# Gates and branch projections of a mixer: from features on the partitions to tokens on the partitions

## The chip, the cores and the metric

One core of a Trainium2 chip runs the whole program. The metric is the device time of one execution in microseconds; the time of a kernel is the median of its runs.

## The reference

The model has three blocks on 256 tokens of width 1024, all in float32. The change lies in the third, whose mixer adds up four branches, each projected and gated:

```python
h = _rms_norm(x, norm_mix_pre[l])
(a_q, a_k, a_v, f_q, f_k, f_v, f_g, c_u, s_x, s_b, s_c) = jnp.split(h @ w_in[l], cuts, axis=-1)
...
ya = (_rms_norm(ya, diff_norm[l]) * (1.0 - lambda_init)).reshape(B, S, BR_W)
...
c_a, c_g = jnp.split(c_u + b_glu[l], 2, axis=-1)
yc = _dwconv_causal(c_a * jax.nn.sigmoid(c_g), conv_dw[l]) + conv_dw_b[l]
yc = jax.nn.silu(_layer_norm(yc, conv_ln_g[l], conv_ln_b[l]))

ys = s_b * _dwconv_causal(s_c * s_x, sc_w[l])

br = jnp.stack([ya, yf, yc, ys], axis=2)
proj = jnp.einsum('bsnc,ncd->bsnd', br, w_branch[l])
gates = jax.nn.sigmoid(h @ w_gate[l] + b_gate[l]).reshape(B, S, N_BRANCH, D)
mixed = jnp.sum(gates * proj, axis=2) @ w_out[l]
x = x + _rms_norm(mixed, norm_mix_post[l])
```

Lines of three dots stand for what is left out: the two attentions that give `ya` and `yf`. Each branch is 512 wide (BR_W), D is 1024; `w_gate` is 1024x4096, split into four gates of 1024, and `w_branch` is 4x512x1024. The branches are counted n = 0 to 3 in the order of the stack, so the convolution is n = 2.

## The kernel before, in words

All weights come from one array in the order in which they are used (`weight_order`). A chunk is 1 MB in two pieces of 128x1024; `feed` loads pieces on SP's queue some pieces ahead. Products are exact to float32: `prepare` rounds each piece to a high half on ScalarE (`whi`, line 156), the rest to a low half on VectorE (`wlo`, line 162), and `mm3` (lines 235 to 237) multiplies high by high, low by high and high by low. How far ahead pieces are prepared is limited by `nprep` (11 in this stage) past twice the chunks that `done()` has counted.

Nothing is scheduled by the compiler: the order of the instructions on each engine is the order in which the program writes them. A step of work on TensorE ends with a `tick`, which writes, in this order, the `whi` of the next piece, one step of each generator in `lanes` and `light`, the `wlo` of that piece, and some steps of `slow`. With lanes alive or fewer than three pieces waiting one piece is prepared in a tick, otherwise two; `slow` advances by three steps, by one if lanes are alive or two pieces were prepared, and by one after a branch.

There are two ways to multiply. `ws` keeps the weights as the stationary operand, 128 output features, and streams the 256 tokens: the result has features on the partitions. `as_` keeps 128 tokens as the stationary operand and streams 512 features of weights: the result has tokens on the partitions. `as_pair` runs a pair of chunks through `as_`, first for the one half of the tokens and then for the other, and calls `evac` for each half; it ticks four times, and counts its chunks as done in the second half.

The stage in question runs over MIX_STEPS. `gates(j)` computes two gate tiles of 128 features by `ws_chunk` (48 matmuls of 256 columns); ScalarE takes them out of PSUM with Sigmoid, the bias being a value of each partition (line 1183). `branches(j0)` projects four tiles of 128 features with one chunk; for each two of them VectorE multiplies the result in PSUM with the gates (lines 1205 and 1207) and adds it up in `part` (line 1208). With the last branch, n = 2, the sum is split into high and low half for the product with `w_out_2`, whose stationary operand has features on the partitions. PSUM results live in a pool of four banks (`bank`), the weights and most activations in a pool of 43 buffers of 4 KB (`b4`).

Beside it, VectorE works through the convolution: `conv_taps` in `slow`, 31 taps on each of four tiles, two tiles at a time (line 860). After the fifth branch chunk `conv_lane` is started, which waits for the taps to run out, transposes the result on TensorE, normalizes it on VectorE, transposes it back, applies Silu on ScalarE and splits it: that is branch n = 2. After the sixth, `mem_norm` loads the memory on POOL's queue (`mem_load`), normalizes it and transposes it, for a later stage.

Of the kernel before, what the change touches and what calls it, by code (L numbers as in the profile page):

```python
# [37 lines left out]
PP = {}  # L38
_o = 0
for _n, _w in (("b_glu", 8), ("conv_dw", 4 * 31), ("conv_dw_b", 4), ("ln_g", 4), ("ln_b", 4),  # L40
               ("sc_w", 12), ("b_gate", 32), ("ffn_dw", 3 * 44), ("ffn_dw_b", 44)):
    PP[_n] = _o
    _o += _w
NPP = _o
# [55 lines left out]
def tile_model(ctx: ExitStack, tc: tile.TileContext, order, wall, x, mem, gains, pparam, rparam, w_fg,  # L100
# [721 lines left out]
    def ppc(name, i, n=1):  # L822
        return pp[:, PP[name] + i:PP[name] + i + n]
# [317 lines left out]


    sbt = None
    for i in range(4):
        if i % 2 == 0:
            sbt = t2("sb")
            ws_chunk(("colsat", "w_in_2", S_B + i * 128), lambda ps: nc.scalar.activation(sbt, ps, AF.Copy))

        def shortconv(ps, i, sbt):
            sx = t1("sx")  # L1150
            nc.scalar.activation(sx, ps[:, 0:256], AF.Copy)
            nc.vector.tensor_tensor(sx, ps[:, 256:512], sx, op=ALU.mult)
            y = t1("sy")
            k0 = PP["sc_w"] + i * 3
            nc.vector.tensor_scalar(y, sx, pp[:, k0 + 2:k0 + 3], None, op0=ALU.mult)
            for s in (1, 2):
                nc.vector.scalar_tensor_tensor(y[:, s:256], sx[:, 0:256 - s], pp[:, k0 + 2 - s:k0 + 3 - s], y[:, s:256],
                                               op0=ALU.mult, op1=ALU.add)
            yield
            if i == 0:  # L1160
                br(3)
            nc.vector.tensor_tensor(y, y, sbt[:, (i % 2) * 256:(i % 2) * 256 + 256], op=ALU.mult)
            split(brh[3][:, i, :], brl[3][:, i, :], y)

        def evac(ps):
            lane(shortconv(ps, i, sbt))

        ws_chunk(("list256", "w_in_2", S_X + i * 128, S_C + i * 128), evac)


    gbuf, part, mx = {}, [], {}
    state["branch"] = 0

    def gates(j):

        if j // 2 % 2 == 0:
            gbuf["tile", j // 4] = b4([128, 4, 256], "gates")
        tile = gbuf["tile", j // 4]

        def evac(ps):  # L1180
            for f in range(2):
                n, ft = GATE_ORDER[j + f]
                nc.scalar.activation(tile[:, (j + f) % 4, :], ps[:, f * 256:f * 256 + 256], AF.Sigmoid, bias=ppc("b_gate", n * 8 + ft))
        ws_chunk(("gates", j), evac)

    def branches(j0, count=4):

        if j0 % 4 == 0:
            gbuf["w"] = weights(("branch", j0))
        w = gbuf["w"]  # L1190
        for j in range(j0, j0 + count):
            n, ft = GATE_ORDER[j]
            if j % 2 == 0:
                gbuf["ps"] = bank("ps_br")
            ps = gbuf["ps"][:, (j % 2) * 256:(j % 2) * 256 + 256]
            ws(ps, w, (j % 4) * 128, lambda k: brh[n][:, k, :], lambda k: brl[n][:, k, :], width=512)
            if j % 4 == 3:
                done()
            if j % 2 == 0:
                continue  # L1200
            g = gbuf["tile", j // 4].rearrange("p a b -> p (a b)")[:, (j % 4 - 1) * 256:(j % 4 + 1) * 256]
            ft -= 1
            m = part[ft // 4].rearrange("p a b -> p (a b)")[:, ft % 4 * 256:ft % 4 * 256 + 512]
            if n == 0:
                nc.vector.tensor_tensor(m, gbuf["ps"], g, op=ALU.mult)
            else:
                nc.vector.tensor_tensor(g, gbuf["ps"], g, op=ALU.mult)
                nc.vector.tensor_tensor(m, m, g, op=ALU.add)
            if n == 2:
                a = mx[ft // 2] = act_pair()  # L1210
                split(a[0], a[1], tiles(m, 256))
            tick(taps=1)


    mth, mtl, memn = {}, {}, []
# [28 lines left out]

    for kind, j in MIX_STEPS:
        if kind == "gate":
            gates(j)
            if j == 6:
                drain(*lanes, *light)
                part.extend(b4([128, 4, 256], f"part{i}") for i in range(2))  # L1250
            if j == 30:
                drain(cl)
        else:
            branches(j)
            if j == 16:
                cl = lane(conv_lane())
            if j == 20:
                ml = lane(mem_norm(mem_load()))
    drain(ml)
    acc = [pair("mix0"), pair("mix1")]  # L1260
    items = [(weights(("rows2", "w_out_2", c)), *mx.pop(c)) for c in range(4)]


    xk = {}
# [156 lines left out]

GATE_ORDER = [(n, ft + f) for ft in range(0, 8, 2) for n in (0, 1, 3) for f in range(2)] + [(2, ft) for ft in range(8)]
MIX_STEPS = [("gate", 0), ("gate", 2), ("gate", 4), ("gate", 6)]
for _c in range(6):
    MIX_STEPS += [("branch", 4 * _c)] + [("gate", 4 * _c + 8 + _i) for _i in (0, 2) if 4 * _c + 8 + _i < 24]
MIX_STEPS += [("gate", _j) for _j in (24, 26, 28, 30)] + [("branch", 24), ("branch", 28)]


def weight_order():
# [37 lines left out]

    for kind, j in MIX_STEPS:  # L1470
        if kind == "gate":
            o.append(("gates", j))
        else:
            o.append(("branch", j))
    o.extend(("rows2", "w_out_2", c) for c in range(4))
# [18 lines left out]
def _chunk(inp, key):  # L1494
# [24 lines left out]
    if kind == "ffn512":  # L1519
# [1 line left out]
        w = inp["w_up_2"][c * 512:c * 512 + 512]  # L1521
        w = np.concatenate([w[:, n * 256:n * 256 + 256], w[:, D_FF2 + n * 256:D_FF2 + n * 256 + 256]], axis=1)
        return w.reshape(4, 128, 512).transpose(1, 0, 2)
    if kind == "gates":
        w = np.concatenate([inp["w_gate_2"][:, n * 1024 + ft * 128:n * 1024 + ft * 128 + 128]
                            for n, ft in GATE_ORDER[key[1]:key[1] + 2]], axis=1)
        return w.reshape(8, 128, 256).transpose(1, 0, 2)
    if kind == "branch":
        w = np.concatenate([inp["w_branch_2"][n, :, ft * 128:ft * 128 + 128]
                            for n, ft in GATE_ORDER[key[1]:key[1] + 4]], axis=1)  # L1530
        return w.reshape(4, 128, 512).transpose(1, 0, 2)
    raise KeyError(key)


def _layout(inp):

    def per(v):
        return v.reshape(-1, 128).T

    def taps(w):  # L1540
        k, c = w.shape
        return w.reshape(k, c // 128, 128).transpose(2, 1, 0).reshape(128, -1)

    pparam = np.concatenate([per(inp["b_glu_2"]), taps(inp["conv_dw_2"]), per(inp["conv_dw_b_2"]),
                             per(inp["conv_ln_g_2"]), per(inp["conv_ln_b_2"]), taps(inp["sc_w_2"]),
                             per(inp["b_gate_2"]), taps(inp["ffn_dw_2"]), per(inp["ffn_dw_b_2"])], axis=1)
    rparam = np.concatenate([inp[n] for n in ("b_fgt_2", "diff_norm_2", "lam_q1_2", "lam_q2_2", "lam_k1_2",
                                              "lam_k2_2")])[None, :]
    gains = np.stack([inp[n] for n in GAINS])
    return gains, pparam, rparam, inp["w_in_2"][:, F_G:F_G + 8]  # L1550


# [36 lines left out]
```

## Time and profile before

| | us |
|---|---|
| three runs: median (lowest to highest) | 1264.73 (1264.48 to 1264.80) |
| the profiled execution, its own time | 1264.71 |
| its span, first to last instruction | 1263.0 |
| TensorE busy | 1237.4 (98%) |
| VectorE busy | 877.7 (69%) |
| ScalarE busy | 678.4 (54%) |
| GpSimd busy | 9.3 (1%) |
| TensorE's granted clock, mean | 0.999 |

The busy times come from one profiled execution. Matmuls overlap in the pipeline: a matmul of 256 columns is shown with 283 ns although the next one starts 120 ns after it, so the pace is read from the starts. A wait is given in brackets at the end of a line of the timeline, with the engine and the tile that ended it.

### The profile page before, as it was taken

How to read it: one execution, taken by the hardware profiler on the slowest of the kernel's cores; microseconds unless marked ns; L12 is line 12 of the kernel's file. 1: busy time of each engine (PE TensorE's matmuls, PEld its weight loads, DVE VectorE, ACT ScalarE, POOL GpSimd, SP SyncE). 2: the span in 40 equal slices, each digit the busy share in tenths (PEclk: the TensorE clock that was granted, in tenths of full speed). 3: DMA queues.
4: the chain of work that ended last, by engine and by line, in shares of the span. 5: the costliest groups of instructions: out<-in, count | busy, mean ns of one | idle time of the engine just before them, and what ended most of it. 6: DMA issues, size and time to landing. Idle time of an engine off the chain costs nothing. (4 is left out here: it accounts for less than half of the span.)

```text
span 1263.0 us, 20014 instructions
## 1 busy us (share of the span) xinstructions
PE 1237.4 (98%) x7870; PEld 1115.1 (88%) x7870; DVE 877.7 (69%) x1537; ACT 678.4 (54%) x1103; POOL 9.3 (1%) x22
## 2 busy tenths in 40 slices
PE   6999999999999999999999999999999999999997
PEld 4888888899988888899998999899999897899996
DVE  6774768755566766765557578688877877588773
ACT  5553445644444765654444545754446575666552
POOL 0000000000000000000000000000000000000000
PEclk9999999999999999999999999999999999999999
DMA  9765564665664535566565644255665564455530
GB/s 342 279 186 156 159 218 166 213 196 178 198 217 134 183 120 180 187 214 190 179 211 181 208 144 141 71 174 170 188 203 197 182 207 163 159 191 185 183 117 34
DMA packets 64206, 227.43 MB, mean 180 GB/s; under 512 B 8048, under 2 KB 8304, under 8 KB 64112
## 3 DMA queue, kind: packets, MB, share of 16 engines
q1 hardware_dynamic: 61808, 217.76, 52.8%
q0 software_dynamic: 2304, 8.39, 2.0%
q8 instruction: 62, 1.02, 0.3%
q14 instruction: 32, 0.26, 0.1%
HBM read 225.08 MB, written 1.05 MB: 179 GB/s over the span
## 5 line engine op out<-in xcount | busy, mean ns | idle before, releaser
L162 DVE TENSOR_TENSOR wlo<-raw,whi 128x1024 fp32r<-128x1024 f32 x406 | 480.1, 1220 | 79.9 <-ACT whi L156 78.8
L156 ACT ACTIVATE whi<-raw 128x1024 fp32r<-128x1024 f32 x406 | 406.8, 1049 | 52.8 <-PE ps_ws L237 14.8
L235 PE MATMUL ps_ws<-xhi,whi 128*128 128x256 f32 x1376 | 391.3, 284 | 1.2 <-ACT fpT L1126 0.9
L236 PE MATMUL ps_ws<-xlo,whi 128*128 128x256 f32 x1376 | 389.3, 283 | 0.0
L237 PE MATMUL ps_ws<-xhi,wlo 128*128 128x256 f32 x1376 | 389.3, 283 | 0.0
L235 PEld LDWEIGHTS ps_ws<-xhi,whi 128*128 128x128 f32 x1376 | 263.8, 192 | 5.9 <-issue 2.5
L236 PEld LDWEIGHTS ps_ws<-xlo,whi 128*128 128x128 f32 x1376 | 263.9, 192 | 1.5
L237 PEld LDWEIGHTS ps_ws<-xhi,wlo 128*128 128x128 f32 x1376 | 263.9, 192 | 0.0
L235 PE MATMUL ps_as<-whi,xhi 128*128 128x512 f32 x352 | 142.2, 404 | 0.3 <-ACT xhi L231 0.3
L236 PE MATMUL ps_as<-wlo,xhi 128*128 128x512 f32 x352 | 137.7, 391 | 0.5 <-DVE wlo L162 0.5
L237 PE MATMUL ps_as<-whi,xlo 128*128 128x512 f32 x352 | 138.1, 392 | 0.0
L268 PE MATMUL mlp<-wlo,act 128*128 128x512 f32 x240 | 93.7, 390 | 0.0
L267 PE MATMUL mlp<-whi,act 128*128 128x512 f32 x240 | 93.5, 390 | 0.0
L237 PEld LDWEIGHTS ps_as<-whi,xlo 128*128 128x128 f32 x352 | 66.2, 188 | 15.3 <-DVE xlo L232 1.1
L236 PEld LDWEIGHTS ps_as<-wlo,xhi 128*128 128x128 f32 x352 | 66.5, 189 | 14.2 <-DVE wlo L162 1.3
L235 PEld LDWEIGHTS ps_as<-whi,xhi 128*128 128x128 f32 x352 | 66.4, 189 | 13.6 <-ACT xhi L231 0.9
L662 DVE SCALAR_TENSOR_TENSOR relu<-ps_ws,relu 128x512 f32<-128x512 f32 x24 | 16.6, 691 | 87.1 <-ACT relu L661 87.1
L661 ACT ACTIVATE relu<-ps_ws 128x512 f32<-128x512 f32 x24 | 14.4, 598 | 113.8 <-PE ps_ws L237 113.8
L271 PE MATMUL mlp<-whi,act 128*128 128x512 f32 x240 | 73.9, 389 | 0.0
L271 PEld LDWEIGHTS mlp<-whi,act 128*128 128x128 f32 x240 | 45.1, 188 | 9.5
L267 PEld LDWEIGHTS mlp<-whi,act 128*128 128x128 f32 x240 | 45.2, 188 | 8.6
L268 PEld LDWEIGHTS mlp<-wlo,act 128*128 128x128 f32 x240 | 45.2, 188 | 8.6
(427 smaller groups left out, 1613.8 us busy)
## 6 DMA issues: line engine op xcount, KB each, us to landing
raw<-in_wall_dram SPq DMA_DIRECT2D x406, 512.0 KB, 4.2
h<-in_x_dram SPq DMA_DIRECT2D x4, 256.0 KB, 5.7
gainln_mix_post<-in_gains_dram POOLq DMA_DIRECT2D x2, 512.0 KB, 5.6
gainln_mlp_pre<-in_gains_dram POOLq DMA_DIRECT2D x2, 512.0 KB, 6.7
gainln_mlp_post<-in_gains_dram POOLq DMA_DIRECT2D x2, 512.0 KB, 7.6
mem<-in_mem_dram POOLq DMA_DIRECT2D x2, 512.0 KB, 5.8
out_dram<-h SPq DMA_DIRECT2D x4, 256.0 KB, 2.9
dec<-in_t_dec_dram SPq DMA_DIRECT2D x2, 384.0 KB, 8.9
```

The lines of the kernel that those rows point to most:

```text
L156: nc.scalar.activation(hi, raw, AF.Copy)
L162: nc.vector.tensor_tensor(lo, raw, hi.bitcast(F32), op=ALU.subtract)
L235: nc.tensor.matmul(o, ah, bh, start=start, stop=False)
L236: nc.tensor.matmul(o, ah, bl, start=False, stop=False)
L237: nc.tensor.matmul(o, al, bh, start=False, stop=stop)
L267: nc.tensor.matmul(acc[t][n], ah[:, k, ts], wh[k][:, ns], start=st, stop=False)
L268: nc.tensor.matmul(acc[t][n], ah[:, k, ts], wl[k][:, ns], start=False, stop=False)
L271: nc.tensor.matmul(acc[t][n], al[:, k, ts], wh[k][:, ns], start=False, stop=False)
L661: nc.scalar.activation(r, ps, AF.Relu)
L662: nc.vector.scalar_tensor_tensor(r, ps, 0.0, r, op0=ALU.max, op1=ALU.mult)
```

## The change

The gates and the branch projections change from `ws` to `as_`. A gate group is now 512 features of one branch for 256 tokens, from two chunks, by `as_pair`; a branch group is 512 features of one branch from one chunk. The number of chunks is the same, 16 and 8, and so is the order of gates and branches; `GATE_ORDER` now names halves of 512 features instead of tiles of 128.

With the features in the free dimension, the gate's bias is no longer one value for each partition. It comes as a row, broadcast to 128 partitions by a DMA on POOL's queue (`gate_bias`, two groups for each DMA; the rows stand behind the gains in `gains`), VectorE adds it while it takes the result out of PSUM, and ScalarE applies Sigmoid in SBUF. VectorE multiplies the projection with the gate as before, now for one half of the tokens at a time; the additions into `part` go to GpSimd. For the product with `w_out_2` the sum has to have features on the partitions: `mixed` transposes it on TensorE, four tiles of 128x128 for each half of the tokens and of the features, and splits it out of PSUM. It is put into `light` and runs one tick later.

```diff
@@ -1141,7 +1141,17 @@
 
 
     sbt = None
+    gbias = {}
+
+    def gate_bias(j):
+
+        b = gbias[j // 2] = b4([128, 2, 512], "gate_bias")
+        r = len(GAINS) + j // 2
+        nc.gpsimd.dma_start(b, gains[r:r + 1, :].rearrange("a (n c) -> a n c", n=2).broadcast_to([128, 2, 512]))
+
     for i in range(4):
+        if i == 2:
+            gate_bias(0)
         if i % 2 == 0:
             sbt = t2("sb")
             ws_chunk(("colsat", "w_in_2", S_B + i * 128), lambda ps: nc.scalar.activation(sbt, ps, AF.Copy))
@@ -1168,48 +1178,50 @@
         ws_chunk(("list256", "w_in_2", S_X + i * 128, S_C + i * 128), evac)
 
 
-    gbuf, part, mx = {}, [], {}
-    state["branch"] = 0
-
-    def gates(j):
-
-        if j // 2 % 2 == 0:
-            gbuf["tile", j // 4] = b4([128, 4, 256], "gates")
-        tile = gbuf["tile", j // 4]
-
-        def evac(ps):
-            for f in range(2):
-                n, ft = GATE_ORDER[j + f]
-                nc.scalar.activation(tile[:, (j + f) % 4, :], ps[:, f * 256:f * 256 + 256], AF.Sigmoid, bias=ppc("b_gate", n * 8 + ft))
-        ws_chunk(("gates", j), evac)
-
-    def branches(j0, count=4):
-
-        if j0 % 4 == 0:
-            gbuf["w"] = weights(("branch", j0))
-        w = gbuf["w"]
-        for j in range(j0, j0 + count):
-            n, ft = GATE_ORDER[j]
-            if j % 2 == 0:
-                gbuf["ps"] = bank("ps_br")
-            ps = gbuf["ps"][:, (j % 2) * 256:(j % 2) * 256 + 256]
-            ws(ps, w, (j % 4) * 128, lambda k: brh[n][:, k, :], lambda k: brl[n][:, k, :], width=512)
-            if j % 4 == 3:
+    gbuf, part, mx = {}, {}, {}
+
+    def gate_group(j):
+
+        if j % 2 == 0 and j < 6:
+            gate_bias(j + 2)
+        tile = gbuf[j] = b4([128, 2, 512], "gates")
+
+        def evac(t, ps):
+            nc.vector.tensor_tensor(tile[:, t, :], ps, gbias[j // 2][:, j % 2, :], op=ALU.add)
+            nc.scalar.activation(tile[:, t, :], tile[:, t, :], AF.Sigmoid)
+
+        as_pair([("cols512", "w_gate_2", 2 * GATE_ORDER[j][1] + GATE_ORDER[j][0], c) for c in range(2)], evac)
+
+    def branch_group(j):
+
+        f, n = GATE_ORDER[j]
+        w = weights(("branch", j))
+        g = gbuf.pop(j)
+        if n == 0:
+            part[f] = b4([128, 2, 512], "part")
+        m = part[f]
+        for t in range(2):
+            ps = bank("ps_br")
+            as_(ps, w, brh[n], brl[n], t, True, True)
+            if n == 0:
+                nc.vector.tensor_tensor(m[:, t, :], ps, g[:, t, :], op=ALU.mult)
+            else:
+                nc.vector.tensor_tensor(g[:, t, :], ps, g[:, t, :], op=ALU.mult)
+                nc.gpsimd.tensor_tensor(m[:, t, :], m[:, t, :], g[:, t, :], op=ALU.add)
+            if t == 1:
                 done()
-            if j % 2 == 0:
-                continue
-            g = gbuf["tile", j // 4].rearrange("p a b -> p (a b)")[:, (j % 4 - 1) * 256:(j % 4 + 1) * 256]
-            ft -= 1
-            m = part[ft // 4].rearrange("p a b -> p (a b)")[:, ft % 4 * 256:ft % 4 * 256 + 512]
-            if n == 0:
-                nc.vector.tensor_tensor(m, gbuf["ps"], g, op=ALU.mult)
-            else:
-                nc.vector.tensor_tensor(g, gbuf["ps"], g, op=ALU.mult)
-                nc.vector.tensor_tensor(m, m, g, op=ALU.add)
             if n == 2:
-                a = mx[ft // 2] = act_pair()
-                split(a[0], a[1], tiles(m, 256))
+                if t == 0:
+                    mx[2 * f], mx[2 * f + 1] = act_pair(), act_pair()
+                later(lambda t=t: mixed(f, t))
             tick(taps=1)
+
+    def mixed(f, t):
+        pt = bank("ps_mx")
+        transposes(pt, part[f][:, t, :])
+        for c in range(2):
+            a = mx[2 * f + c]
+            split(a[0][:, :, tok(t)], a[1][:, :, tok(t)], tiles(pt[:, c * 256:c * 256 + 256]))
 
 
     mth, mtl, memn = {}, {}, []
@@ -1244,21 +1256,20 @@
 
     for kind, j in MIX_STEPS:
         if kind == "gate":
-            gates(j)
-            if j == 6:
+            gate_group(j)
+            if j == 1:
                 drain(*lanes, *light)
-                part.extend(b4([128, 4, 256], f"part{i}") for i in range(2))
-            if j == 30:
+            if j == 7:
                 drain(cl)
         else:
-            branches(j)
-            if j == 16:
+            branch_group(j)
+            if j == 4:
                 cl = lane(conv_lane())
-            if j == 20:
+            if j == 5:
                 ml = lane(mem_norm(mem_load()))
     drain(ml)
     acc = [pair("mix0"), pair("mix1")]
-    items = [(weights(("rows2", "w_out_2", c)), *mx.pop(c)) for c in range(4)]
+    items = [(weights(("rows2", "w_out_2", c)), *mx[c]) for c in range(4)]
 
 
     xk = {}
@@ -1421,11 +1432,11 @@
 
 
 
-GATE_ORDER = [(n, ft + f) for ft in range(0, 8, 2) for n in (0, 1, 3) for f in range(2)] + [(2, ft) for ft in range(8)]
-MIX_STEPS = [("gate", 0), ("gate", 2), ("gate", 4), ("gate", 6)]
-for _c in range(6):
-    MIX_STEPS += [("branch", 4 * _c)] + [("gate", 4 * _c + 8 + _i) for _i in (0, 2) if 4 * _c + 8 + _i < 24]
-MIX_STEPS += [("gate", _j) for _j in (24, 26, 28, 30)] + [("branch", 24), ("branch", 28)]
+GATE_ORDER = [(f, n) for f in range(2) for n in (0, 1, 3)] + [(f, 2) for f in range(2)]
+MIX_STEPS = [("gate", 0), ("gate", 1)]
+for _j in range(6):
+    MIX_STEPS += [("branch", _j)] + ([("gate", _j + 2)] if _j < 4 else [])
+MIX_STEPS += [("gate", 6), ("gate", 7), ("branch", 6), ("branch", 7)]
 
 
 def weight_order():
```

## Rows read from the trace of the kernel before

**Rows 1.** The page's first part: busy time, share of the span, instructions by engine.
```profile
PE 1237.4 (98%) x7870; PEld 1115.1 (88%) x7870; DVE 877.7 (69%) x1537; ACT 678.4 (54%) x1103; POOL 9.3 (1%) x22
```

**Rows 2.** Busy times by stretch, gates to `w_out_2`: length, engines, clock, DMA.
```profile
843.40:866.40 23.00, 23.00 (x194) 23.00 (x193) 20.37 (x37) 11.29 (x17) 0.00 (x0) 1.00 0.58 178
866.40:929.60 63.20, 63.20 (x529) 63.20 (x528) 53.47 (x87) 27.18 (x36) 0.00 (x0) 1.00 0.60 179
929.60:986.40 56.80, 56.26 (x468) 55.61 (x468) 40.90 (x69) 33.77 (x55) 2.09 (x4) 1.00 0.59 200
```

**Rows 3.** Timeline, TensorE, in a gate chunk: start, length, engine, line, what.
```profile
950.09 0.28 PE L237 MATMUL ps_ws<-xhi,wlo 128*128 128x256 f32 x1
950.21 0.28 PE L235 MATMUL ps_ws<-xhi,whi 128*128 128x256 f32 x1
```

**Rows 4.** Timeline, TensorE, retention stage: twelve 512-column matmuls, then four transposes between such.
```profile
60.00 0.39 PE L235 MATMUL ps_as<-whi,xhi 128*128 128x512 f32 x1
...
62.72 0.39 PE L235 MATMUL ps_o<-vh,ph 128*128 128x512 f32 x1
...
66.81 0.60 PE L294 MATMUL ps_ot<-ident,og 128*128 128x128 f32 x4
67.16 0.48 PE L235 MATMUL ps_as<-whi,xhi 128*128 128x512 f32 x1
67.48 0.40 PE L236 MATMUL ps_as<-wlo,xhi 128*128 128x512 f32 x1
```

**Rows 5.** Instructions on tile `part`: count, min/median/max ns, first and last start.
```profile
L1205 DVE TENSOR_TENSOR part<-ps_br,gates x4: 684/684/693, 870.9 to 941.6; 128x512 f32<-128x512 f32 x4
L231 ACT ACTIVATE act<-part x4: 632/632/634, 980.0 to 992.8; 128x512 fp32r<-128x512 f32 x4
```

**Rows 6.** Timeline, VectorE, within one cycle of two gate chunks and a branch chunk.
```profile
890.98 0.68 DVE L1205 TENSOR_TENSOR part<-ps_br,gates 128x512 f32<-128x512 f32 x1
891.58 1.22 DVE L162 TENSOR_TENSOR wlo<-raw,whi 128x1024 fp32r<-128x1024 f32 x1
...
897.37 1.23 DVE L162 TENSOR_TENSOR wlo<-raw,whi 128x1024 fp32r<-128x1024 f32 x1 [1.92 <-ACT whi L156]
...
903.12 1.23 DVE L162 TENSOR_TENSOR wlo<-raw,whi 128x1024 fp32r<-128x1024 f32 x1 [1.14 <-ACT whi L156]
904.27 1.21 DVE L860 SCALAR_TENSOR_TENSOR yc<-cu,pp,yc 128x236 f32<-128x236 f32 x3
```

**Rows 7.** Timeline, ScalarE, end of one gate chunk in that cycle.
```profile
901.31 0.84 ACT L1183 ACTIVATE gates<-ps_ws,pp 128x256 f32<-128x256 f32 x2 [3.02 <-PE ps_ws L237]
902.04 2.00 ACT L156 ACTIVATE whi<-raw 128x1024 fp32r<-128x1024 f32 x2
```

**Rows 8.** Timeline, VectorE, layer norm of the convolution and norm of `mem`.
```profile
949.58 0.69 DVE L873 BATCH_NORM_STATS2 bs<-ps_ct 128x6 f32<-128x512 f32 x1
...
954.94 2.35 DVE L162 TENSOR_TENSOR wlo<-raw,whi 128x1024 fp32r<-128x1024 f32 x2
960.55 1.29 DVE L232 TENSOR_TENSOR brl<-cxn,brh 128x512 fp32r<-128x512 f32 x2 [3.26 <-ACT brh L231]
...
962.89 0.15 DVE L1229 TENSOR_TENSOR memss<-memss 128x2 f32<-128x2 f32 x1
...
966.31 1.41 DVE L1234 SCALAR_TENSOR_TENSOR mem<-mem,z_mem,gainnorm_mem 128x512 f32<-128x512 f32 x2
```

**Rows 9.** Timeline, ScalarE, the convolution's Silu.
```profile
955.80 1.28 ACT L887 ACT_TABLE_LOAD   x1
957.09 2.90 ACT L887 ACTIVATE cxn<-ps_ct,pp 128x128 f32<-128x128 f32 x8
```

**Rows 10.** Timeline, VectorE: work of the first gate tick, and the last taps.
```profile
849.64 1.22 DVE L162 TENSOR_TENSOR wlo<-raw,whi 128x1024 fp32r<-128x1024 f32 x1
...
928.71 0.81 DVE L860 SCALAR_TENSOR_TENSOR yc<-cu,pp,yc 128x226 f32<-128x226 f32 x2
```

**Rows 11.** Groups by line, GpSimd (shape, count, busy us, mean ns, idle before).
```profile
masks.py:199 POOL TENSOR_SCALAR_AFFINE_SELECT ident<-ident 128x128 f32<-128x128 f32 x1 | 0.3, 289 | 0.1
```

More of the change, by code (lines that the diff above doesn't have):

```diff
@@ L40 @@
 for _n, _w in (("b_glu", 8), ("conv_dw", 4 * 31), ("conv_dw_b", 4), ("ln_g", 4), ("ln_b", 4),
-               ("sc_w", 12), ("b_gate", 32), ("ffn_dw", 3 * 44), ("ffn_dw_b", 44)):
+               ("sc_w", 12), ("ffn_dw", 3 * 44), ("ffn_dw_b", 44)):
     PP[_n] = _o
@@ L1471, in weight_order @@
         if kind == "gate":
-            o.append(("gates", j))
+            two("cols512", "w_gate_2", 2 * GATE_ORDER[j][1] + GATE_ORDER[j][0])
         else:
@@ L1523, in _chunk @@
         return w.reshape(4, 128, 512).transpose(1, 0, 2)
[L1524 to L1527, printed above, removed]
     if kind == "branch":
-        w = np.concatenate([inp["w_branch_2"][n, :, ft * 128:ft * 128 + 128]
-                            for n, ft in GATE_ORDER[key[1]:key[1] + 4]], axis=1)
-        return w.reshape(4, 128, 512).transpose(1, 0, 2)
+        f, n = GATE_ORDER[key[1]]
+        return inp["w_branch_2"][n, :, f * 512:f * 512 + 512].reshape(4, 128, 512).transpose(1, 0, 2)
     raise KeyError(key)
@@ L1545, in _layout @@
                              per(inp["conv_ln_g_2"]), per(inp["conv_ln_b_2"]), taps(inp["sc_w_2"]),
-                             per(inp["b_gate_2"]), taps(inp["ffn_dw_2"]), per(inp["ffn_dw_b_2"])], axis=1)
+                             taps(inp["ffn_dw_2"]), per(inp["ffn_dw_b_2"])], axis=1)
     rparam = np.concatenate([inp[n] for n in ("b_fgt_2", "diff_norm_2", "lam_q1_2", "lam_q2_2", "lam_k1_2",
                                               "lam_k2_2")])[None, :]
-    gains = np.stack([inp[n] for n in GAINS])
+    b_gate = inp["b_gate_2"].reshape(4, 2, 512)
+    rows = [inp[n] for n in GAINS] + list(np.stack([b_gate[n, f] for f, n in GATE_ORDER]).reshape(4, 1024))
+    gains = np.stack(rows)
     return gains, pparam, rparam, inp["w_in_2"][:, F_G:F_G + 8]
```

## Prediction

> **What bounds the kernel now.** I read first the busy line of the page [rows 1]: TensorE is busy for 98% of the span, so a stage costs what its matmuls cost, unless another engine makes TensorE wait. Then the stage that the change touches, from the first gate matmul to the first matmul with `w_out_2` [rows 2]: 143.0 us, in which TensorE lacks 0.54 us, at a granted clock of 1.00 (the 2.4 GHz level), while VectorE is busy for 114.8 us and ScalarE for 72.2. VectorE is the second engine, and not evenly: 20.4 of 23.0 us, 53.5 of 63.2, 40.9 of 56.8. Last I read its order of work. Four streams share its queue there: the low halves of the weights (`wlo`, one of 1.22 us for each piece), the 31 convolution taps for each channel tile, the gated products, and near the end the convolution's layer norm with the norm of `mem`. What ends its idle time is `whi` of ScalarE [rows 6], which stands behind the sigmoids that wait for TensorE [rows 7]. So VectorE has slack today because the gates leave PSUM by ScalarE alone.
>
> Times below count from 843.4 us, the first gate matmul (the first branch matmul at 866.4 less four chunks of 5.76).
>
> **TensorE's part.** Before, a chunk is 48 matmuls of 256 columns, started every 0.12 us [rows 3]: 5.76 us, and 24 chunks (16 gate, 8 branch) take 138.24. After, a chunk is 24 matmuls of 512 columns; twelve such take 2.72 us, 0.2267 each [rows 4], so 24 chunks take 130.6. Removed: 7.7 us. Added are four groups of four transposes. The group in [rows 4] holds the queue for 0.35 us, and the matmul behind it takes 0.32 instead of 0.23: 0.44 each, 1.8 in all. Net gain 5.9 us, all of it on the engine that sets the end. The rows show 0.12 and 0.227 us from start to start. The Trainium skill ("TensorE: Matmul & The Clock Gate", Back-to-back issue gap) gives N/2.4 + 2.5 ns, 109 and 216 ns: as an estimate from it, 125.8 us against 124.3, a gain that the transposes would eat, and a sum 6 us later than mine. By that rule this trace's matmuls are 5 to 10% too long; the rows disagree with it and leave it no chance here.
>
> **What VectorE gets.** Products: 16 of 128x512 before and after (0.684 us [rows 5]; 0.60 from one start to the next [rows 6]). Removed: 12 additions and 4 low halves of the sum, of the same shape and priced alike, 9.6 us of queue. Added: 16 bias additions out of PSUM, at the product's row, 9.6, and 8 low halves of half that width, 2.6 to 5.2 by the pair of 1.29 in [rows 8]. Net 3 to 5 us in 143, which is little. What counts is the order. The bias addition must wait for TensorE, the sigmoid (0.632 on SBUF, the `act` row of [rows 5], of which 0.53 hold the queue) must wait for the addition, the next `whi` (1.05, two in 2.00 [rows 7]) stands behind the sigmoid, and the next `wlo` behind that `whi`: 1.7 us in which VectorE stands still in its own chain, where before only ScalarE stood still.
>
> One gate group, by the new order: weights are released only in the second half of `as_pair`, so the four ticks prepare 1, 0, 1 and 2 pieces (the limit is 11 pieces past those done) and run 3, 3, 3 and 1 taps. VectorE: 4 `wlo` at 1.14 from start to start, 10 taps at 0.38 (three in 1.21), 2 additions at 0.60, and waits of 0.6 and 1.77 for ScalarE: 12.0 us, against TensorE's 10.88. A branch group: 2 products, 2 `wlo`, 2 taps, 4.2 us against 5.44. A cycle of both: 16.2 against 16.3 (in the old order 14.2 of 17.3, with waits of 1.92 and 1.14 for `whi` [rows 6]). So VectorE never catches up what it is late. It enters late: the `wlo` of the first gate tick starts at 6.2 [rows 10], gate groups 0 and 1 add some 1.1 each, and I find the first product 5.2 us behind its matmuls. That alone costs nothing: a PSUM bank of this pool of four is written again some 11 us after its last matmul (two gate halves or more lie between), and weights are prepared four chunks ahead.
>
> **Where it becomes TensorE's.** In the old order the taps ran out at 928.7, nearly three chunks before the transposes of the layer norm, whose statistics begin at 949.6 [rows 8, 10]; with 12 per cycle instead of 14 the last falls behind branch group 4. Then the layer norm and the norm of `mem` go through the same queue. Along it, with the prices of [rows 6, 8, 9]: product of branch 5 at 100.5 (its matmuls end at 97.9); `wlo`; statistics to `cxn` 5.36; `wlo`; bias addition of gate 6 at 108.6. Now ScalarE: sigmoid, two squares (1.2, at the row of [rows 5]), `whi`, table 1.28, eight Silu 2.9, high half: VectorE waits 7.6 us and goes on at 116.8 (before, it waited 3.3 there [rows 8]). Low halves 1.2, the small operations 2.3, `wlo`: second addition of gate 6 at 121.5, 10 us behind TensorE. Two products for `mem` 1.3, wait 0.5, `wlo`, two more, `wlo`: gate 7 at 127.5. Wait 1.8, `wlo`, wait 0.3, low halves of `mem` 1.2, `wlo`: second addition at 133.6. Wait 2.3, low halves, `wlo`: product of branch 6 at 138.8. Its addition on GpSimd, and the first transposes can start at 140.8.
>
> TensorE without waits would be there at 128.6. It is held in four places: 0.9 for the last tap; 3.9 and 4.4 for PSUM banks that the late additions and low halves release, where `mem` is transposed; 2.9 around branch 6: 12.1 us in all. Less the 0.5 that it waits today, less the 5.9: the kernel becomes 5.6 us slower. The same summing along the old order gives 142.4 for the stage whose rows give 143.0, so I take the method as good to 1 or 2 us.
>
> **GpSimd.** No row shows it adding a tensor. Its price: a DVE addition of this shape, 0.69, from below; the `affine_select` of 128x128 [rows 11], 0.289 us, for two inputs and four times the elements some 1.7 from above. I take 1.2, an estimate; between 0.9 and 2.0 the end moves by 1.6 us. Whether an addition there holds up VectorE: from nothing to its own length, 1.2 us, for each of 12. Put into the chain above, 0.6 each makes it 10.5 slower, 1.2 each 16.9. No row decides; I take a quarter, 0.3, near the lower end, since every `wlo` in [rows 6, 8] has one length, and get about +7.5 to +8. The Trainium skill ("SBUF — State Buffer", Who interferes with whom) speaks for the upper end: a VectorE instruction with two SBUF inputs and a GpSimd instruction that reads SBUF exclude one another, and the second blocks until the first ends. `wlo` and the taps have two SBUF inputs; by that rule the sum would be near 1281, and no row here shows it either way.
>
> **Edits at nothing.** Four bias rows as DMAs on POOL's queue, issued two gate groups (22 us) ahead of their use; additions stand behind them there, and where one of the DMAs waits for its buffer the next addition is a group away. The three `mem` DMAs stand ahead of branch 6's additions by two gate groups. Two more of the 43 buffers are held; that delays a `whi`, which is four chunks ahead. If these covers fail, it is a bank or a weight that comes later still, in the direction of the forecast.
>
> **The sum.** The profiled execution took 1264.71 us, span 1263.0 and 1.71 around it; the median of the three runs is 1264.73. 1264.7 + 5.6 + 2 = 1272.
>
> **Rivals.**
> 1. VectorE keeps up, and TensorE's gain comes through: some waits behind ScalarE are hidden and only branch 6's transposes wait, 0.5 to 1 us. For it: every bank has some 11 us of cover; in the old order VectorE recovered from the layer norm by itself. Against it: the chain above is 12 us too long. It decides at the second addition of gate 6: if that is done by 115 instead of 121.5 (that is, if ScalarE runs the Silu block without the sigmoid and squares ahead), the rest catches up. 1264.7 - 5.9 + 0.8 = 1259.6. Chance 0.13.
> 2. The two cancel: waits of 4 to 8 us. 1262.5 to 1267. Chance 0.11.
> 3. GpSimd holds up VectorE by most of its length, 0.6 to 1.2 us for each addition: +11 to +17, 1276 to 1282. For it: in the first 86 us VectorE has nothing left in which to make up for it. Against it: no row shows one engine lengthening the other. Chance 0.20, with what is over. It is the rule of the Trainium skill cited above.
> 4. The forecast, +3 to +11: 1267 to 1276. Chance 0.56.
>
> **How the numbers follow.** 0.2%, 2.5 us, is about what a measurement of this kernel tells from no change. Faster 0.13 (rival 1), same 0.11 (rival 2), slower 0.76 (forecast and rival 3). The range runs from 1262, which leaves rival 1 out, to 1281, which leaves out the upper end of rival 3.
>
> **What would show it.** Right: matmuls of `ps_as` and `ps_br` at 0.227; in the stage's last 50 us TensorE waiting for VectorE or ScalarE at `pt`, `ps_br` and `ps_mx`, 8 to 20 us in sum; the bias addition of gate 6 over 5 us behind its matmul; VectorE busy for 85% or more. Wrong: TensorE's waits under 3 us there (rival 1). Rival 3: `wlo` or taps beside a GpSimd addition longer than 1.22 us and 1.21 for three, or the product of branch 5 more than 4 us behind its matmuls. The prediction falls if the ticks prepare or tap otherwise than I count, or if PSUM banks are handed out in another order than that of their release.

## The result, and the profile after

The changed kernel takes 1278.27 us (median of four runs, 1277.95 to 1280.1); the kernel before, on the same chip, 1264.65. The ratio is 1.011, with a 95% interval of 1.0098 to 1.0122: 13.6 us slower. The forecast was 1272, that is 7.3 slower, with a range of 1262 to 1281. The profiled execution is the longest of the four, 1280.1 with a span of 1278.3; what is added up from its rows is therefore up to 1.8 us too large.

The page's first part, after (busy us, share of the span, instructions):

```profile
PE 1239.5 (97%) x7310; PEld 1091.6 (85%) x7310; DVE 885.8 (69%) x1545; ACT 674.7 (53%) x1091; POOL 34.5 (3%) x38
```

TensorE is busy for 2 us more than in [rows 1], although its matmuls in the stage should take less. The stage by stretch (length, then the busy time of PE, PEld, DVE, ACT and POOL, the granted clock, the DMA share and GB/s), up to the first matmul with `w_out_2` at 1001.30:

```profile
843.00:866.00 23.00, 23.00 (x107) 19.16 (x105) 18.87 (x35) 9.21 (x12) 0.30 (x1) 1.00 0.52 179
866.00:929.00 63.00, 63.00 (x279) 52.18 (x278) 54.41 (x79) 27.77 (x32) 9.66 (x6) 1.00 0.58 199
929.00:1001.30 72.30, 58.01 (x245) 46.26 (x244) 54.08 (x92) 34.33 (x53) 14.87 (x10) 0.88 0.49 165
```

Against [rows 2] the first two stretches are as full as before, and TensorE has no wait in them. In the last it is busy for 58.0 of 72.3 us, and its mean clock is 0.88. VectorE, the second engine of before, is busy for 54 of 63 and 54 of 72 us. The stage, 143.0 us before, takes 157.5 (843.76 to 1001.30). TensorE's waits in it (by whom it waited for: sum, times, longest):

```profile
PE ps_ct L869 <- DVE yc L860: 4.7, 2, 2.6
PE pt L294 <- DVE mtl L232: 3.1, 1, 3.1
PE ps_mx L294 <- POOL part L1210: 2.2, 1, 2.2
PE ps_ct L869 <- DVE gates L1209: 1.9, 1, 1.9
PE pt L294 <- DVE gates L1190: 1.2, 1, 1.2
PE pt L294 <- ACT gates L1191: 1.2, 1, 1.2
```

They add up to 14.3 us, in the places that the prediction named: the transposes of the convolution (6.6), those of `mem` (5.5) and the first of `mixed` (2.2).

Now VectorE, in a cycle late in the second stretch; the [brackets] hold the idle time ahead of an instruction and what ended it:

```profile
878.77 1.22 DVE L162 TENSOR_TENSOR wlo<-raw,whi 128x1024 fp32r<-128x1024 f32 x1
...
885.70 0.69 DVE L1190 TENSOR_TENSOR gates<-ps_as,gate_bias 128x512 f32<-128x512 f32 x1
888.04 2.36 DVE L162 TENSOR_TENSOR wlo<-raw,whi 128x1024 fp32r<-128x1024 f32 x2 [1.65 <-ACT whi L156]
890.31 0.47 DVE L860 SCALAR_TENSOR_TENSOR yc<-cu,pp,yc 128x245 f32<-128x245 f32 x1
890.70 0.69 DVE L1209 TENSOR_TENSOR gates<-ps_br,gates 128x512 f32<-128x512 f32 x1
...
892.43 1.50 DVE L860 SCALAR_TENSOR_TENSOR yc<-cu,pp,yc 128x244 f32<-128x244 f32 x1
...
895.59 1.50 DVE L860 SCALAR_TENSOR_TENSOR yc<-cu,pp,yc 128x244 f32<-128x244 f32 x1
897.01 1.21 DVE L162 TENSOR_TENSOR wlo<-raw,whi 128x1024 fp32r<-128x1024 f32 x1
```

Three things are to be seen. The bias addition at 885.70 is followed by 1.65 us of nothing, until `whi` is through. From the first `wlo` of a gate group (878.77) to the first product (890.70) pass 11.9 us. And the two taps of the branch group (892.43, 895.59), 0.47 us long elsewhere (890.31), take 1.50 each. GpSimd's queue beside it:

```profile
891.52 2.14 POOL L1210 TENSOR_TENSOR part<-part,gates 128x512 f32<-128x512 f32 x1 [12.98 <-DVE gates L1209]
894.61 2.21 POOL L1210 TENSOR_TENSOR part<-part,gates 128x512 f32<-128x512 f32 x1 [0.95 <-DVE gates L1209]
...
950.07 4.34 POOL L1210 TENSOR_TENSOR part<-part,gates 128x512 f32<-128x512 f32 x2 [1.00 <-DVE gates L1209]
954.36 1.09 POOL L1232 DMA_DIRECT2D mem<-in_mem_dram  x2
...
998.82 1.30 POOL L1210 TENSOR_TENSOR part<-part,gates 128x512 f32<-128x512 f32 x1 [4.74 <-DVE gates L1209]
```

Each of the two long taps starts under an addition of GpSimd and ends 0.27 us after it. The addition itself takes 2.14 to 2.21 us there, and 1.30 at 998.82, where VectorE runs nothing with two inputs in SBUF. The row of 954.36 is for later: the loads of `mem`.

Last, VectorE's own milestones from the last product of branch 5 to branch 6:

```profile
950.98 0.68 DVE L1209 TENSOR_TENSOR gates<-ps_br,gates 128x512 f32<-128x512 f32 x1
951.58 1.70 DVE L162 TENSOR_TENSOR wlo<-raw,whi 128x1024 fp32r<-128x1024 f32 x1
953.20 0.69 DVE L873 BATCH_NORM_STATS2 bs<-ps_ct 128x6 f32<-128x512 f32 x1
...
959.83 0.69 DVE L1190 TENSOR_TENSOR gates<-ps_as,gate_bias 128x512 f32<-128x512 f32 x1
968.16 1.29 DVE L232 TENSOR_TENSOR brl<-cxn,brh 128x512 fp32r<-128x512 f32 x2 [7.65 <-issue]
...
972.75 0.68 DVE L1190 TENSOR_TENSOR gates<-ps_as,gate_bias 128x512 f32<-128x512 f32 x1
...
989.92 0.69 DVE L1209 TENSOR_TENSOR gates<-ps_br,gates 128x512 f32<-128x512 f32 x1
```

The 7.65 us ahead of 968.16, for which the profile names no engine, end with the first high half that ScalarE writes behind the Silu; ScalarE worked without a gap from the sigmoid at 960.54 up to there. TensorE waits for VectorE's end of this chain at `mem` and at `mixed`.

### The profile page after: what moved, and what is told of

Its sections match the earlier page's. It is cut to its first block, busy times and chain, and to the rows that moved or that the text cites. A ratio compares the mean times of both kernels' runs of the same rounds, so it can differ in the third digit from the quotient of the medians.

```text
span 1278.3 us, 18950 instructions
## 1 busy us (share of the span) xinstructions
PE 1239.5 (97%) x7310; PEld 1091.6 (85%) x7310; DVE 885.8 (69%) x1545; ACT 674.7 (53%) x1091; POOL 34.5 (3%) x38
## 5 line engine op out<-in xcount | busy, mean ns | idle before, releaser
L235 PE MATMUL ps_ws<-xhi,whi 128*128 128x256 f32 x1120 | 318.7, 285 | 1.2 <-ACT fpT L1126 0.9
L236 PE MATMUL ps_ws<-xlo,whi 128*128 128x256 f32 x1120 | 316.9, 283 | 0.0
L237 PE MATMUL ps_ws<-xhi,wlo 128*128 128x256 f32 x1120 | 316.8, 283 | 0.0
L235 PEld LDWEIGHTS ps_ws<-xhi,whi 128*128 128x128 f32 x1120 | 214.7, 192 | 5.9 <-issue 2.5
L236 PEld LDWEIGHTS ps_ws<-xlo,whi 128*128 128x128 f32 x1120 | 214.8, 192 | 1.5
L237 PEld LDWEIGHTS ps_ws<-xhi,wlo 128*128 128x128 f32 x1120 | 214.7, 192 | 0.0
L235 PE MATMUL ps_as<-whi,xhi 128*128 128x512 f32 x480 | 193.8, 404 | 0.6 <-ACT xhi L231 0.6
L237 PE MATMUL ps_as<-whi,xlo 128*128 128x512 f32 x480 | 189.2, 394 | 0.1
L236 PE MATMUL ps_as<-wlo,xhi 128*128 128x512 f32 x480 | 188.9, 393 | 0.0
L860 DVE SCALAR_TENSOR_TENSOR yc<-cu,pp,yc 128x255 f32<-128x255 f32 (+29 forms) x120 | 57.3, 515 | 0.0
```

Source lines behind the costliest of these rows:

```text
L235: nc.tensor.matmul(o, ah, bh, start=start, stop=False)
L236: nc.tensor.matmul(o, ah, bl, start=False, stop=False)
L237: nc.tensor.matmul(o, al, bh, start=False, stop=stop)
L860: nc.vector.scalar_tensor_tensor(y[:, s:256], u[:, 0:256 - s], w, y[:, s:256], op0=ALU.mult, op1=ALU.add)
```

## Experiments

All times are medians; the ratio is to the kernel before on the same chip, with its 95% interval. The kernel before took 1264.65 to 1264.87 in these comparisons.

| kernel | us | ratio |
|---|---|---|
| after | 1278.27 | 1.0110 (1.0098 to 1.0122) |
| 1 additions on VectorE | 1277.91 | 1.0103 (1.0088 to 1.0118) |
| 2 Sigmoid behind `whi` | 1264.10 | 0.9995 (0.9985 to 1.0005) |
| 3 no bias | 1265.65 | 1.0008 (0.9999 to 1.0018) |
| 4 waits filled with matmuls | 1278.38 | 1.0106 (1.0091 to 1.0121) |
| 5 no additions | 1269.85 | 1.0042 (1.0027 to 1.0057) |
| 6 = 2, additions on VectorE | 1261.52 | 0.9975 (0.9966 to 0.9984) |
| 7 = 2, `mem` in other PSUM banks | 1264.70 | 1.0003 (0.9994 to 1.0012) |
| 8 = 7, loads of `mem` earlier, last additions on VectorE | 1261.50 | 0.9975 (0.9966 to 0.9985) |
| 9 before, Sigmoid behind `whi` | 1264.61 | 0.9998 (0.9989 to 1.0007) |
| 10 = 7, loads of `mem` earlier, all additions on VectorE | 1261.48 | 0.9974 (0.9964 to 0.9985) |

The theory (A) has two parts. VectorE falls behind because the bias addition, the sigmoid, `whi` and `wlo` stand in one chain across two in-order queues; and each addition on GpSimd that meets an instruction of VectorE with both inputs in SBUF costs VectorE about one addition. The rivals: GpSimd costs nothing (B), the amount of VectorE's work decides, not its order (C), the clock that falls behind the waits is the loss (D).

### 1. The additions on VectorE

```diff
-                nc.gpsimd.tensor_tensor(m[:, t, :], m[:, t, :], g[:, t, :], op=ALU.add)
+                nc.vector.tensor_tensor(m[:, t, :], m[:, t, :], g[:, t, :], op=ALU.add)
```

> The twelve additions into part go back to VectorE. Theory A (an addition on GpSimd holds up VectorE: in the trace of after six taps that met one took 1.5 us instead of 0.46 and one wlo 1.70 instead of 1.22, 6.7 us up to branch 5, while eight additions on VectorE would cost 8 x 0.6 = 4.8 us): about 2 to 2.5 us faster than after, 1275.8 (1273.5 to 1277.5). Theory B (GpSimd takes nothing from VectorE, the long taps are a matter of the record): VectorE gets 4.8 us more ahead of the layer norm, 1282 to 1284.

Measured: 1277.91, the same as after within the intervals; both expectations missed. VectorE's timeline:

```profile
941.65 0.68 DVE L1209 TENSOR_TENSOR gates<-ps_br,gates 128x512 f32<-128x512 f32 x1
942.37 0.69 DVE L1210 TENSOR_TENSOR part<-part,gates 128x512 f32<-128x512 f32 x1
942.98 1.22 DVE L162 TENSOR_TENSOR wlo<-raw,whi 128x1024 fp32r<-128x1024 f32 x1
944.12 0.45 DVE L860 SCALAR_TENSOR_TENSOR yc<-cu,pp,yc 128x226 f32<-128x226 f32 x1
...
952.23 0.69 DVE L873 BATCH_NORM_STATS2 bs<-ps_ct 128x6 f32<-128x512 f32 x1
```

The tap is back at 0.45. The addition follows its own product and takes 0.72 us from the product's start to its own, and 0.61 to the next: 0.13 more than the 0.6 I had put in, because it waits for the product. Eight of them are 5.8 us where the hold-ups were 6.7. Counted from the first gate matmul (843.55 here, 843.76 after), the statistics start at 108.7 us, against 109.4 after: 0.8 of these 0.9. So on which engine the additions stand hardly matters as long as VectorE is the late one; an addition on GpSimd is no cheaper for VectorE than doing it itself. That this equality means hold-ups, and not that neither place costs anything, is what run 5 tells.

### 2. The Sigmoid behind `whi`

```diff
+    def behind_whi(f):
+        def g():
+            f()
+            yield
+        light.append(g())
...
             nc.vector.tensor_tensor(tile[:, t, :], ps, gbias[j // 2][:, j % 2, :], op=ALU.add)
-            nc.scalar.activation(tile[:, t, :], tile[:, t, :], AF.Sigmoid)
+            behind_whi(lambda: nc.scalar.activation(tile[:, t, :], tile[:, t, :], AF.Sigmoid))
```

The tick behind the eviction writes `whi` first, then the sigmoid, then `wlo`. No instruction is added or taken away.

> The Sigmoid of a gate half is written behind the whi of its tick instead of ahead of it, nothing else. Theory A (VectorE falls behind in the chain bias addition, sigmoid, whi, wlo, in which it stands still 0.5 and 1.65 us for each gate group, 12.9 us up to branch 5): the waits of TensorE ahead of the layer norm's transposes (6.6 us) go and most of those at mem and branch 6, 1262 (1259 to 1267). Theory B (the additions on GpSimd and the work itself make VectorE late, the stands are idle time anyway): above 1272.

Measured: 1264.10, 14.2 us less than after. VectorE in a gate group, and its first product of branch 6:

```profile
916.97 1.23 DVE L162 TENSOR_TENSOR wlo<-raw,whi 128x1024 fp32r<-128x1024 f32 x1 [0.53 <-ACT whi L156]
...
919.22 0.69 DVE L1197 TENSOR_TENSOR gates<-ps_as,gate_bias 128x512 f32<-128x512 f32 x1
919.83 2.35 DVE L162 TENSOR_TENSOR wlo<-raw,whi 128x1024 fp32r<-128x1024 f32 x2
...
943.23 0.68 DVE L880 BATCH_NORM_STATS2 bs<-ps_ct 128x6 f32<-128x512 f32 x1
...
975.17 0.69 DVE L1216 TENSOR_TENSOR gates<-ps_br,gates 128x512 f32<-128x512 f32 x1 [0.63 <-PE ps_br L244]
```

Behind the second bias addition (919.22) `wlo` now follows without a gap. The statistics start 99.8 us after the first gate matmul (843.45 here), where it was 109.4: the lateness ahead of the layer norm is 9.7 us smaller. At 975.17 VectorE waits for the matmuls of branch 6, where in the changed kernel the product came 2.1 us behind them (the thirteenth starts at 987.82, the product at 989.92). TensorE's waits in the stage:

```profile
PE pt L301 <- DVE mtl L239: 2.2, 1, 2.2
PE ps_mx L301 <- POOL part L1217: 0.6, 2, 0.3
PE pt L301 <- DVE gates L1197: 0.4, 1, 0.4
PE ps_ct L301 <- DVE cxn L885: 0.2, 1, 0.2
```

3.4 us are left of 14.3. The additions are still on GpSimd and still stretch the taps; with the chain broken VectorE has room for it. So the amount of VectorE's work does not decide by itself (C): the same instructions in another order are 14.2 us faster. One thing more came with the edit: a Sigmoid of gate 6 that stood ahead of the convolution's Silu on ScalarE now stands behind it. What that alone is worth no run shows.

### 3. No bias

```diff
-            nc.vector.tensor_tensor(tile[:, t, :], ps, gbias[j // 2][:, j % 2, :], op=ALU.add)
-            nc.scalar.activation(tile[:, t, :], tile[:, t, :], AF.Sigmoid)
+            nc.scalar.activation(tile[:, t, :], ps, AF.Sigmoid)
```

> Leaves out the gates' bias: ScalarE takes the gate out of PSUM with Sigmoid, VectorE has no addition there. Takes away both the chain and 16 x 0.6 us of VectorE's queue. Theory A (the place in the chain costs, not the 9.6 us): within 2 us of the kernel with the sigmoid behind whi, 1259 to 1264. Theory C (the amount of VectorE work decides): 5 us or more below that kernel.

Measured: 1265.65, 1.5 us above run 2, which does the additions, and above the range expected for (A); (C) expected 5 us or more below run 2. TensorE's waits, and ScalarE ahead of them:

```profile
PE pt L294 <- ACT gates L1190: 3.9, 1, 3.9
PE ps_mx L294 <- POOL part L1209: 1.1, 2, 0.9
952.11 0.63 ACT L1238 ACTIVATE sqm<-mem 128x512 f32<-128x512 f32 x1 [11.01 <-DMA mem<-in_mem_dram]
```

ScalarE stands 11.0 us for the loads of `mem`, and the sigmoid for which TensorE then waits comes out of the work that piled up behind them. In run 2 it stands 7.0 us for the same loads. Both kernels are held there, so what 9.6 us less of VectorE's work could bring without this wait run 3 does not show. Against (C) stands run 2, and run 6 below, which puts the twelve additions on VectorE and is faster than run 2.

### 4. Matmuls in the waits

```diff
+    def warm(n, st, mv):
+        ...
+        for _ in range(n):
+            nc.tensor.matmul(wt[0], st[:, 0, 0:128], mv[:, 0:2, :].rearrange("p a b -> p (a b)"), start=True, stop=True)
...
             for i in range(4):
+                if t == 0 and i != 1:
+                    warm(8, xh2[0], xh2[0])
                 nc.tensor.transpose(pts[t][:, i * 128:i * 128 + 128], yc[:, i, tok(t)], ident)
```

(and 5, 5 and 12 ahead of the transposes of `mem`, 9 ahead of the first `mixed`).

> Additional matmuls of 128x512 into an unused bank stand where TensorE waits in after (8, 8 and 8 around the taps' transposes, 5, 5 and 12 at mem, 9 at the first mixed), each group somewhat shorter than its wait. Theory A (VectorE's queue sets the end from the layer norm to branch 6; the fallen clock lies beside its waits and costs only the 1.6 us behind the first transposes of mixed): 1276.5 (1275 to 1278.5). Theory D (the matmuls at half clock behind the waits, 6.3 us in the records, are lost time): 1271 to 1273.

The windows of TensorE after (length, busy, granted clock), where it first stands in short pieces and then works again:

```profile
945.00:950.00 5.00, 1.09 (x4) 0.52 0.25 65
950.00:955.00 5.00, 5.00 (x15) 0.50 0.16 65
```

The clock is at the lower level, 1.2 GHz, there; it fell in the second of three waits of 1.9, 2.1 and 2.6 us with a few transposes between. The twelve matmuls that follow start 0.43 us apart instead of 0.23. Counted in the records, 23 such matmuls (0.2 us too long each) and 13 slow transposes make some 6 us of the stage. With the waits filled:

```profile
945.00:950.00 5.00, 3.81 (x19) 1.00 0.28 93
950.00:955.00 5.00, 5.00 (x24) 1.00 0.05 17
```

The clock stays at 2.4 GHz here (it still falls once, around the first transposes of `mem`), and the kernel takes 1278.38: no difference. So (D) is refuted. The slow matmuls lay beside work of VectorE that was late anyway: counted from the first gate matmul (843.26 here), the product of branch 6 starts at 146.1 us as against 146.2 after. The one place where the path runs through them in the trace is behind the first transposes of `mixed` (six matmuls and four transposes at the lower clock, some 1.6 us), and even of that nothing showed in the median, though the stage of the profiled execution is 1.3 us shorter (156.3 for 157.5).

### 5. No additions

```diff
-                nc.gpsimd.tensor_tensor(m[:, t, :], m[:, t, :], g[:, t, :], op=ALU.add)
+                pass
```

> Leaves out the twelve additions into part; all else as in after. Theory A (each addition on GpSimd that meets a two-input VectorE instruction in SBUF holds it up: 6.7 us ahead of the layer norm, on the path from there on, and the 1.3 us of the addition ahead of the first transposes of mixed): 1270 to 1272. Theory B (the additions hold up nothing that matters, as the unmoved time with the additions on VectorE might also mean): 1276 to 1278.5.

Measured: 1269.85, 8.4 us less than after, as (A) expected. VectorE's timeline, for the same branch group as above and at the statistics:

```profile
890.07 0.69 DVE L1209 TENSOR_TENSOR gates<-ps_br,gates 128x512 f32<-128x512 f32 x1
...
891.80 0.47 DVE L860 SCALAR_TENSOR_TENSOR yc<-cu,pp,yc 128x244 f32<-128x244 f32 x1
...
946.66 0.69 DVE L873 BATCH_NORM_STATS2 bs<-ps_ct 128x6 f32<-128x512 f32 x1
```

The tap takes 0.47, and the statistics start 103.5 us after the first gate matmul (843.14 here), 5.9 us earlier than in the changed kernel; six taps of 1.04 and a `wlo` of 0.48 too much are 6.7, of which some turned into waits for `whi`. This is against (B). The other 2.5 answer to the addition of 2.2 us that stood ahead of the first transposes; that share is argued. (The transposes here no longer depend on the product of branch 6 either. It ends at 983.87 and they start at 984.04, so that cost nothing.)

### 6. Sigmoid behind `whi`, additions on VectorE

Runs 1 and 2 together.

> Sigmoid behind whi and the additions on VectorE. With VectorE no longer late the place of the additions is a matter of 12 x 0.7 us on VectorE against seven hold-ups of 1.05: the same within 1 us as the kernel with the sigmoid alone behind whi (1264.1), perhaps 1 us faster since the loads of mem no longer stand behind four additions on GpSimd (ScalarE stood 7.0 us for them): 1263 to 1264.5. If the additions on VectorE were dearer than on GpSimd: 1266 or more.

Measured: 1261.52, faster than the kernel before by 0.25% and than run 2 by 2.6 us, more than expected. TensorE's waits:

```profile
PE ps_ct L301 <- DVE cxn L885: 0.9, 2, 0.7
PE ps_mx L301 <- DVE part L1217: 0.8, 2, 0.6
PE pt L301 <- DVE mtl L239: 0.5, 1, 0.5
```

The wait at `mem` shrank from 2.6 us to 0.5. Two things changed at once: the hold-ups, and the loads of `mem`, which no longer stand behind four additions on GpSimd's queue (ScalarE stands 2.4 us for them, for 7.0 in run 2). Runs 2 and 6 alone do not part the two; run 8 does in part.

### 7. The transposes of `mem` in other PSUM banks

```diff
-            to_T(memn[t], t, mth, mtl)
+            to_T(memn[t], t, mth, mtl, pair(f"memT{t}"))
```

> Sigmoid behind whi, and the transposes of mem write into the four PSUM banks of the other pool, which nothing uses in this stage. The waits of TensorE at these transposes (0.43 and 2.16 us) and the slow matmuls behind the second go; VectorE had 0.6 and 0.9 us to spare at branch 6, so up to 1 us comes back there: 1261.5 (1260.5 to 1262.5).

Measured: 1264.70, no gain over run 2 and above the expected range. The waits at `mem` are gone, and all of them stand at one other place:

```profile
PE ps_mx L301 <- POOL part L1217: 4.4, 1, 4.4
```

VectorE gives out the product of branch 6 when its own queue comes to it; a free bank only lets TensorE arrive earlier and wait there. ScalarE in the same run shows what holds that queue up:

```profile
947.77 0.63 ACT L1246 ACTIVATE sqm<-mem 128x512 f32<-128x512 f32 x1 [6.99 <-DMA mem<-in_mem_dram]
```

It stands 7.0 us for the loads of `mem`, which were issued behind the additions of branches 4 and 5; the Silu of the convolution stands behind it, and VectorE behind that.

### 8 and 10. The loads of `mem` earlier

```diff
+            if j == 4:
+                gm = mem_load()
             branch_group(j)
...
-                ml = lane(mem_norm(mem_load()))
+                ml = lane(mem_norm(gm))
```

Both have the Sigmoid behind `whi` and the banks of run 7. In run 8 only the last four additions are on VectorE, in run 10 all twelve.

> As the one before, with the loads of mem issued ahead of branch 4's additions, and the last four additions (branches 6 and 7) on VectorE, 0.7 us instead of 1.3 on GpSimd ahead of the transposes of mixed: 1260.3 (1259.5 to 1262); TensorE's floor by the sum of the prediction is 1258.8.

> Sigmoid behind whi, all additions on VectorE, loads of mem issued ahead of branch 4's additions, transposes of mem in the unused PSUM banks. Of the kernel with the first two (1261.5), 0.5 us of waits at mem can go, and may come back at branch 6 as they did with the banks alone: 1261.0 (1260.3 to 1262).

Measured: 1261.50 and 1261.48; with run 6 three ways to the same time. The earlier loads with four additions moved give 3.2 us over run 7; which of the two gave it no run parts. Run 8 still has eight additions on GpSimd, and they still hold up VectorE:

```profile
889.58 1.49 DVE L867 SCALAR_TENSOR_TENSOR yc<-cu,pp,yc 128x243 f32<-128x243 f32 x1
```

Run 10 has none there and takes the same time. With the chain broken the hold-ups ahead of the layer norm thus cost the kernel nothing; they cost it where VectorE is late. In run 10 the banks and the earlier loads give nothing over run 6, the first expectation's 0.5 us included: TensorE's waits are 2.4 us in sum, at `ps_mx` and at the second transposes of the convolution, where in run 6 they were 2.2.

### 9. The kernel before, with the same reordering

The edit of run 2, at the Sigmoid of `gates`.

> The kernel before, with the same reordering: the Sigmoids of a gate tile behind the whi of their tick. Theory A (the order matters only where VectorE stands in the gate's own path; before, TensorE lacks 0.54 us in the stage, so nothing is to be had): 1264.7, within 0.8. If writing whi first were a gain by itself: below 1263.

Measured: 1264.61, no difference. The order is no gain by itself: in the kernel before, where TensorE lacks 0.54 us in the stage, there is nothing for it to win. In the changed kernel the eviction is a step of VectorE's and the sigmoid stands between it and the next `whi`, and there it is worth 14.2 us.

## Why the prediction came out as it did

The sign, the place and the mechanism held; the size did not. It fell where rival 3 had put it (+11 to +17), and that is where the price of GpSimd's additions decided, the one term for which the trace of before had no row.

- TensorE's part: right. Eighteen chunks run without a wait from 843.76 to 941.73, 5.44 us each, as summed; a group of transposes costs 0.44 among matmuls.
- One gate group on VectorE: 12.0 forecast, 11.9 measured, with waits of 0.49 and 1.65 for the 0.6 and 1.77.
- One branch group: 4.2 forecast; 4.25 without additions (874.52 to 878.77), 6.3 with them (890.70 to 897.01). This is the failing term, 1.03 for each addition that met a tap, where I had taken 0.3 for each of the twelve.
- My reason for 0.3 was wrong, not only its size: "since every `wlo` in [rows 6, 8] has one length" argues from stretches in which GpSimd does nothing. Such rows say nothing on contention, and the value should have been left at the middle of its bounds or above.
- What follows was right by its own working, 6.7 to 7.5 us later. Forecast from 843.4, so measured less 843.76: the second product of branch 5 at 107.2 for 100.5; the bias addition of gate 6 at 116.1 for 108.6; VectorE's wait for ScalarE's Silu 7.65 for 7.6; the second addition of gate 6 at 129.0 for 121.5; the product of branch 6 at 146.2 for 138.8. The lateness of the branch groups goes through the layer norm, the Silu and `mem` unreduced, and comes out at TensorE.
- Run 5 lacks the hold-ups and the last addition of 1.2: 4.4 us slower by the sum, 5.1 measured. That they are close is in part luck, since TensorE's waits there are 6.9 us for the 10.9 summed, and slow matmuls, which the sum has not, stand for the rest.
- The end: the first transposes at 149.2 for 140.8, since this addition too met a `wlo` (2.2 us, for the 1.2 that I took and the 1.30 that it takes alone).
- TensorE's waits by place: 0.9, 8.3 and 2.9 forecast, 6.6, 5.5 and 2.2 measured. The sum of 12.1, with the additions' 2, is close to 14.3, and that is luck: 14.3 of waits, less the 0.5 of before and the 5.9 gained, would make the kernel 7.9 us slower, not 13.6. The other 6 are TensorE's slow matmuls, which fill time that it would have waited for VectorE. Where the waits lie was wrong at the convolution, whose taps are what the additions stretch.
- The clock was not priced at all. TensorE's records got 6 us longer by it, and run 4 shows that this cost nothing here, because VectorE was the late one behind these waits. The prediction had no reason for leaving it out.
- "Edits at nothing": wrong for `mem`. I put its loads ahead of branch 6's additions and overlooked that they stand behind those of branches 4 and 5. They were issued at 954.36, at 944.65 in the kernel before, and ScalarE stood for them; in the slow kernel that hid behind VectorE (run 1 issues them at 941.96 and gains nothing by it), in runs 2, 3 and 7 it was next in line.
- Rival 1 (1259.6) was decided where the prediction said, at the second addition of gate 6: 129.0, not under 115. Runs 6, 8 and 10 come within 2 us of its time once the chain is broken, so TensorE's gain was there all the time.

The row of "what would show it" that parted the forecast from rival 3, taps beside an addition and the product of branch 5 more than 4 us behind its matmuls, said rival 3: 9 us (941.73 to 950.98). Of the signs for the forecast, TensorE's pace and its waits came; VectorE busy for 85% or more did not: it is busy for 126.6 us of the stage's 157.5, 80%.

That an addition of GpSimd and a VectorE instruction with both inputs in SBUF exclude one another is what the Trainium skill says ("SBUF — State Buffer", Who interferes with whom). The trace agrees, with 1.50 us for a tap of 0.47. The same section says that a VectorE instruction with at most one input in SBUF, outside the modes that use both ports, is free of it; the trace agrees there too: the product that reads PSUM takes 0.68 us at 950.98, in the middle of two additions. The time by that rule was near 1281 in the prediction, nearer to the 1278.27 than mine.

## What to carry to other kernels

When an eviction moves from one engine to another, write down what stands behind it in both in-order queues: here the same instructions in another order, with the Sigmoid behind the next weights' rounding, were worth 14.2 us, more than leaving out the twelve additions altogether (8.4). A step that is handed to GpSimd is not off VectorE's queue if both read two tensors from SBUF at that time; count it at about its own length in VectorE's chain (here 1.03 us of 1.29) until a trace with both engines at work shows otherwise. Whether that costs the kernel anything depends on VectorE being late, as runs 8 and 10 show. And a wait that is taken away at its symptom comes back elsewhere: filling TensorE's waits or giving it free banks changed nothing as long as the queues of VectorE and ScalarE were late.

## What the runs showed of the hardware

- An addition of 128x512 in float32 takes GpSimd 1.26 to 1.30 us with no such instruction of VectorE beside it, and 2.1 to 2.2 beside `wlo`: the one of 891.52 ends 1.14 us after the `wlo` that was running when it started, and the next tap ends 0.27 us after the addition.
- The granted clock of TensorE is 1.00 up to 944.20, through a wait of 1.9 us and two transposes, 0.74 on average over the next wait (944.20 to 946.28), and 0.50 from there to 955.20. It fell again in the wait of 3.1 us at `mem`, and at the first transposes of `mixed`, after a wait of 2.2 us: these four hold the queue for 0.73 us instead of 0.35.
- In this kernel, whose VectorE is late, the granted clock and the length of matmuls are no measure of loss: run 4 raised the mean clock from 0.993 to 0.997 and changed nothing in the median.
